# A gated three-branch layer: merge gates and branch projections from feature-major to token-major, and another order of the first transfers

## The chip, the cores and the metric

The kernel runs on one core of one Trainium2 chip. A core has TensorE (matmuls into the accumulators of PSUM), VectorE (DVE), ScalarE (ACT), GpSimd (POOL) and SyncE (SP), which here issues DMAs; 16 DMA engines move data between HBM and SBUF. The metric is the device time of one execution in microseconds (us). Several runs are taken, and their median is compared.

## The reference, cut to what matters

The layer has d = 1024 features and 256 tokens. After the input projection each branch has its output, the branches are projected, weighted by sigmoid gates and summed, and one more projection and a residual add follow.

```python
h = rms_norm(x, norm_g)
(qa, ka, va, ga, ub, vb, gb, qc, gc, ma, mb, mc) = split_cols(h @ w_in, IN_SPLITS)
out_a = moba_attention(qa, ka, va) * silu(ga)          # 6 heads of 128, causal
out_b = gmlp_spatial_gate(ub, vb, gmlp_ln_g, w_spatial, b_spatial) * silu(gb)
out_c = memory_cross_attention(qc, mem_n, w_mem_kv) * silu(gc)
y = (sigmoid(ma) * (out_a @ w_branch_a)                # ma, mb, mc: 1024 columns each
     + sigmoid(mb) * (out_b @ w_branch_b)
     + sigmoid(mc) * (out_c @ w_branch_c))
x = x + y @ w_out
return rms_norm(x, final_norm_g)
```

## The kernel before

All weights are float32. Each is split into two rounded parts, hi and lo, and a product is made of three matmuls, hi x hi, hi x lo and lo x hi (`mm3`, L271 to L274), which sum into one accumulator. Activations are split in the same way (hh and hl of x times its gain, nh and nl of the normalised x, ah/al, obh/obl, och/ocl of the branches, yh and yl of y).

The weights come as pieces of 1 MB (`raw`, three buffers), all from SP's queue, and one piece is two chunks of 128 x 1024. `split` makes a chunk's hi on ScalarE (L129) and its lo on VectorE (L133), three chunks ahead of their use (`LEAD`), into four buffers of each. The main loop (L765) runs over all chunks; in each step it lets small units of work in (`U.slot`, L60: a unit runs when its predecessors are done for `gap` chunks and its cost fits the room of each engine), splits a chunk, loads a piece and issues the chunk's matmuls. The order of the instructions on each engine is the order in which this loop writes them.

There are two kinds of chunk. A "fea" chunk (`mm_fea`, L335) makes 128 output features for all 256 tokens: the weights are the stationary operand, the activations move, and 24 matmuls are 256 wide. A "tok" chunk (`mm_tok`, L286) makes part of 512 output features for two token halves of 128: the activations are stationary, the weights move, 12 matmuls are 512 wide, and four chunks fill two accumulators. Before the change the values (`vvb`, three groups of four chunks) and the memory's values (`mv`) are tok chunks, and everything else in the input projection is fea: among it the merge gates, 24 chunks called `sig` (L256, L375). The branch projections (`mm_br`, L693) take two chunks for each 128 features j of y: the sums over six, six and four blocks of the three branches, 48 matmuls of 256; VectorE multiplies each sum by its gate (L710), POOL and VectorE add (L715), and `split2` makes yh and yl. The output projection (`mm_out`, L723) needs y with features on the partitions.

PSUM has eight banks here: four `acc`, for the chunks, and four `aux`, for the units and the end.

At the start x (transposed) and the first four chunks of weights come in blocks k = 0 to 7 of 768 columns (`load_st`, L156), the first one in two parts with the gains. ScalarE makes hi of each block (L236) and hh (L224; for k = 0 VectorE, L234), VectorE makes hl (L227) and lo (L240). Five passes over a zero tile (L186) run on TensorE before the first data. Behind these blocks SP asks for piece 2, for x token-major (`xk`, L173) and then for the further pieces. The row sums of squares of `xk` (`xsq`, L202), the root (`xrow`) and its broadcast over the partitions by a matmul with a diagonal (`xrms`, L219) come while chunks 4 to 7 run; the accumulators of the vvb groups wait for it, since their eviction (`evict_v`, L317) multiplies by it, and POOL then scales x for nh and nl (L410).

Of the kernel before, what the change touches and what calls it, by code (L numbers as in the profile page):

```python
# [78 lines left out]
def tile_hybrid_layer(ctx: ExitStack, tc: tile.TileContext, xw, memT, mem, x, fin_g, ln_g, w, w_sp, b_sp, rope, out):  # L81
# [73 lines left out]

    def load_st(k, a, b):  # L156
        o = 0 if k == 0 and a == 0 else NG + k * XW + a
        e = NG + k * XW + b
        d = 0 if k < 4 else NG + 4 * XW
        nc.sync.dma_start(st[k // 4][:, o - d:e - d], xw[:, o:e])  # L160
# [12 lines left out]
    nc.sync.dma_start(V["xk"], x)  # L173
# [10 lines left out]
    wp = bank()  # L184
    for i in range(5):
        nc.tensor.matmul(wp, warm[:, 0:128], warm, start=True, stop=True)  # L186
# [44 lines left out]
    for k in range(KD):  # L231
        c, a, g = k // 2, (k % 2) * 512, gain[:, k:k + 1]
        if k == 0:
            nc.vector.tensor_scalar(hh[:, k, :], x_k(k), g, None, op0=OP.mult)  # L234
        for o, e in (((0, 256), (256, 512)) if k == 0 else ((0, 512),)):
            nc.scalar.activation(hi[c][:, a + o:a + e], st_k(k, S + o, S + e), AF.Copy)  # L236
# [49 lines left out]
    def mm_tok(c):  # L286
        _, name, o, k0 = chunks[c]
        sh, sl = (V["mh"], V["ml"]) if name == "mv" else (hh, hl)
        if k0 == 0:
            acc[name, o] = [acc_bank(), acc_bank()]  # L290
        for i in range(2):
            k = k0 + i
            if c < 4:

                parts = (((hh, hi, 0, 256), (hh, hi, 256, 512)) if k == 0 else ((hh, hi, 0, 512),)) \
                    + ((hl, hi, 0, 512), (hh, lo, 0, 512))
                for n, (src, wt, a, b) in enumerate(parts):
                    for t in range(2):
                        nc.tensor.matmul(acc[name, o][t][:, a:b], src[:, k, tsl(t)],
                                         wt[c][:, i * 512 + a:i * 512 + b], start=k + n == 0,  # L300
                                         stop=k == KD - 1 and n == len(parts) - 1)
# [33 lines left out]
    def mm_fea(c):  # L335
# [28 lines left out]
        elif name in ("ga", "gc"):  # L364
            if h == 0:
                slot_tile(name, [128, HA if name == "ga" else HC, S], name)
            nc.scalar.activation(V[name][:, h, :], p, AF.Silu)
        elif name == "gb":
            g = sq_tile()
            nc.scalar.activation(g, p, AF.Silu)  # L370
            nc.gpsimd.tensor_tensor(V["ub"][:, h, :], V["ub"][:, h, :], g, OP.mult)
        else:
            if h % 12 == 0:
                slot_tile(f"sig{h // 12}", [128, 12, S], f"p{1 + h // 12}")
            nc.scalar.activation(V[f"sig{h // 12}"][:, h % 12, :], p, AF.Sigmoid)  # L375
# [315 lines left out]
    BR = [("a", k) for k in range(HA)] + [("b", k) for k in range(GB)] + [("c", k) for k in range(HC)]  # L691

    def mm_br(c):  # L693
        _, j, part = chunks[c]
        if j == 0 and part == 0:
# [3 lines left out]
        src = {"a": (V["ah"], V["al"], HA, 0), "b": (V["obh"], V["obl"], GB, 1),  # L699
               "c": (V["och"], V["ocl"], HC, 2)}  # L700
        for i in range(KD):
            br, k = BR[part * KD + i]
            sh, sl, n, gi = src[br]
            if k == 0:
                acc[br] = acc_bank()[:, 0:S]
            mm3(acc[br], hi[c][:, hsl(i)], lo[c][:, hsl(i)], sh[:, k, :], sl[:, k, :], k == 0, k == n - 1)
            if k == n - 1:
                s = gi * KD + j
                sig = V[f"sig{s // 12}"][:, s % 12, :]
                nc.vector.tensor_tensor(sig, acc[br], sig, OP.mult)  # L710
                if br == "a":
                    acc["y"] = sig
                else:
                    eng = nc.gpsimd if br == "b" else nc.vector
                    eng.tensor_tensor(sig, acc["y"], sig, OP.add)  # L715
                    acc["y"] = sig
        if part == 1:
            split2(acc["y"], V["yh"][:, j, :], V["yl"][:, j, :])

# [166 lines left out]
```

## Time and profile before

| | |
|---|---|
| median of 3 runs | 338.62 us (338.11 to 338.70) |
| the profiled execution | 338.83 us, span 337.1 us |
| moved by DMA | 62.98 MB, mean 187 GB/s |
| 24 sigmoid evictions (L375) | first at 196.5, last at 262.7 us, 0.383 us each |
| 24 products with the gates (L710) | from 265.2 to 308.8 us, 0.418 us each |
| matmuls of the gates and the branches | 40 chunks of 24, 256 wide |

The span runs from the first to the last instruction of the profiled execution. In the lists below a row of the timeline is start, duration, engine, line, operation and tiles, a count and, in brackets, how long the engine stood idle before and what ended that. Matmuls overlap: their cost is read from the distance between starts. Busy shares of PE say little for the same reason.

### The profile page before, as it was taken

The numbers are of one execution on the slowest core, as the hardware profiler recorded it, in microseconds if no ns is written. First come the engines' busy times: TensorE is split into PE (matmuls) and PEld (weight loads), VectorE is DVE, ScalarE is ACT, GpSimd is POOL, SyncE is SP. The second block draws the span as 40 slices with busy tenths as digits, with TensorE's granted clock in tenths as the row PEclk, the third lists the DMA queues.
The fourth block names the chain that finished last, engine by engine and source line by source line (L and its number), as shares of the span: only waits on it lengthen the run. The fifth ranks groups of instructions, "written<-read, shape, count | busy, mean of one in ns | idle before, by whom it ended". The sixth has DMA issues, their size and how long they took to land.

```text
span 337.1 us, 6042 instructions
## 1 busy us (share of the span) xinstructions
PE 328.1 (97%) x2461; PEld 313.9 (93%) x2461; DVE 223.1 (66%) x352; ACT 193.0 (57%) x334; POOL 45.8 (14%) x50
## 2 busy tenths in 40 slices
PE   7999999999999999999999999999999999999992
PEld 4886899999999999988999999999999999999882
DVE  3846949978957898678694655444444677776552
ACT  4859669657775666546964564444444452534333
POOL 0006410000001090100035420000000001011022
PEclk9999999999999999999999999999999999999998
DMA  7988993554443372543656246455454635455003
GB/s 238 406 355 294 372 350 131 192 202 160 165 157 127 124 252 64 199 152 135 246 160 232 93 159 192 183 172 206 145 230 143 231 125 192 183 172 203 3 0 124
DMA packets 10732, 62.98 MB, mean 187 GB/s; under 512 B 1200, under 2 KB 1584, under 8 KB 4176
## 3 DMA queue, kind: packets, MB, share of 16 engines
q1 hardware_dynamic: 10704, 62.60, 51.7%
q8 instruction: 19, 0.31, 0.4%
q14 instruction: 9, 0.07, 0.1%
HBM read 61.55 MB, written 1.05 MB: 186 GB/s over the span
## 4 chain that ended last, share of the span: by engine, by line
PE 89%; DMA 5%; ACT 3%; DVE 1%; issue 1%; SPq 0%; DVEq 0%; ACTq 0%
PE acc L272 26%; PE acc L274 26%; PE acc L273 26%; DMA raw<-in_w_dram 4%; PE aux L272 2%; PE aux L273 2%; PE aux L274 2%; DMA st<-in_xw_dram 2%; PE aux L461 1%; ACT hi L129 1%; PE aux L630 1%; ACT jx L202 0%; SPq L160 0%; PE aux L501 0%; PE aux L534 0%
## 5 line engine op out<-in xcount | busy, mean ns | idle before, releaser
L133 DVE TENSOR_TENSOR lo<-raw,hi 128x1024 fp32r<-128x1024 f32 x102 | 128.3, 1260 | 74.5 <-ACT hi L129 74.0
L272 PE MATMUL acc<-nh,hi 128*128 128x256 f32 x496 | 141.3, 285 | 0.0
L274 PE MATMUL acc<-nh,lo 128*128 128x256 f32 x496 | 140.6, 283 | 0.0
L273 PE MATMUL acc<-nl,hi 128*128 128x256 f32 x496 | 140.6, 283 | 0.0
L129 ACT ACTIVATE hi<-raw 128x1024 fp32r<-128x1024 f32 x102 | 107.3, 1053 | 15.2 <-PE aux L274 5.1
L273 PEld LDWEIGHTS acc<-nl,hi 128*128 128x128 f32 x496 | 95.3, 192 | 0.0
L272 PEld LDWEIGHTS acc<-nh,hi 128*128 128x128 f32 x496 | 95.3, 192 | 0.0
L274 PEld LDWEIGHTS acc<-nh,lo 128*128 128x128 f32 x496 | 95.2, 192 | 0.0
L375 ACT ACTIVATE sig<-acc 128x256 f32<-128x256 f32 x24 | 9.2, 383 | 35.2 <-PE acc L274 35.2
L142 ACT ACTIVATE yh<-sig 128x256 fp32r<-128x256 f32 x8 | 3.3, 418 | 23.3 <-DVE sig L715 23.3
L715 POOL TENSOR_TENSOR sig<-sig 128x256 f32<-128x256 f32 x4 | 3.0, 740 | 86.7 <-DVE sig L710 86.7
L639 POOL TENSOR_TENSOR qk<-qk,ga 128x512 f32<-128x512 f32 x3 | 4.0, 1332 | 71.7 <-ACT qk L535 71.7
L272 PE MATMUL acc<-obh,hi 128*128 128x256 f32 x48 | 13.6, 284 | 0.0
L274 PE MATMUL acc<-ah,lo 128*128 128x256 f32 x48 | 13.6, 284 | 0.0
L273 PE MATMUL acc<-al,hi 128*128 128x256 f32 x48 | 13.6, 284 | 0.0
L274 PE MATMUL acc<-obh,lo 128*128 128x256 f32 x48 | 13.6, 284 | 0.0
L272 PE MATMUL acc<-ah,hi 128*128 128x256 f32 x48 | 13.6, 284 | 0.0
L273 PE MATMUL acc<-obl,hi 128*128 128x256 f32 x48 | 13.6, 284 | 0.0
L272 PE MATMUL acc<-hi,hh 128*128 128x512 f32 x32 | 12.7, 397 | 0.6 <-ACT vb L332 0.6
L273 PE MATMUL acc<-lo,hh 128*128 128x512 f32 x32 | 12.5, 391 | 0.0
L274 PE MATMUL acc<-hi,hl 128*128 128x512 f32 x32 | 12.5, 390 | 0.0
L710 DVE TENSOR_TENSOR sig<-acc,sig 128x256 f32<-128x256 f32 x24 | 10.1, 420 | 2.4 <-PE acc L274 2.4
(196 smaller groups left out, 583.6 us busy)
## 6 DMA issues: line engine op xcount, KB each, us to landing
raw<-in_w_dram SPq DMA_DIRECT2D x50, 1024.0 KB, 4.8
st<-in_xw_dram SPq DMA_DIRECT2D x7, 384.0 KB, 6.4
raw<-in_w_dram SPq DMA_DIRECT2D x2, 512.0 KB, 9.7
xk<-in_x_dram SPq DMA_DIRECT2D x1, 1024.0 KB, 10.7
mt<-in_memT_dram SPq DMA_DIRECT2D x2, 512.0 KB, 6.9
mm<-in_mem_dram SPq DMA_DIRECT2D x2, 512.0 KB, 8.4
out_dram<-xk SPq DMA_DIRECT2D x2, 384.0 KB, 2.5
fing<-in_fin_g_dram SPq DMA_DIRECT2D x1, 512.0 KB, 5.8
```

The costliest lines, as they stand in the source:

```text
L129: nc.scalar.activation(hi[c][:, a:b], raw[c // 2][:, o + a:o + b], AF.Copy)
L133: nc.vector.tensor_tensor(lo[c][:, a:b], raw[c // 2][:, o + a:o + b], hi[c][:, a:b].bitcast(F32), OP.subtract)
L142: nc.scalar.activation(dh, src, AF.Copy)
L272: nc.tensor.matmul(p, s_hi, m_hi, start=first, stop=False)
L273: nc.tensor.matmul(p, s_hi, m_lo, start=False, stop=False)
L274: nc.tensor.matmul(p, s_lo, m_hi, start=False, stop=last)
L375: nc.scalar.activation(V[f"sig{h // 12}"][:, h % 12, :], p, AF.Sigmoid)
L461: nc.tensor.transpose(p[:, hsl(j)], src, ident)
L630: nc.tensor.matmul(pv[:, a, t, :], V["vb"][:, t, hsl(g)], wsp[:, g, :], start=True, stop=True)
L639: nc.gpsimd.tensor_tensor(src, src, g, OP.mult)
L710: nc.vector.tensor_tensor(sig, acc[br], sig, OP.mult)
L715: eng.tensor_tensor(sig, acc["y"], sig, OP.add)
```

## The change

It has two parts. In the first, the gates become six tok groups of four chunks, whose eviction is one sigmoid of 512 columns for each token half, and the branch projections become token-major as well: two halves of 512 features, eight chunks each, with two accumulators for each branch and 12 matmuls of 512 in a chunk. y then has tokens on the partitions; a new unit `y_split` turns it by transposes on TensorE, two units for each half, and splits it from PSUM. POOL takes no part in the sums any more. In the second part the first transfers are issued by SP and ScalarE in turn, the blocks lie one behind another in HBM, piece 3 is asked for ahead of `xk`, seven passes run instead of five, VectorE makes hh for k = 0 to 3, the third vvb group takes two aux banks, and the costs and gaps of three units change.

```diff
-    load_st(0, 0, S + 256)
-    load_st(0, S + 256, XW)
-    for k in range(1, KD):
-        load_st(k, 0, XW)
+    load_st(nc.sync, 0, 0, S + 256)
+    load_st(nc.scalar, 0, S + 256, XW)
+    load_st(nc.sync, 1, 0, XW)
+    load_st(nc.scalar, 2, 0, XW)
+    for k in range(3, KD):
+        load_st(nc.sync, k, 0, XW)
     raw_alloc(2)
     load_part(2, 0, CH)
     load_part(2, CH, PIECE)
+    load(3)
...
-    for i in range(5):
+    for i in range(7):
         nc.tensor.matmul(wp, warm[:, 0:128], warm, start=True, stop=True)
...
-        if k == 0:
+        if k < 4:
             nc.vector.tensor_scalar(hh[:, k, :], x_k(k), g, None, op0=OP.mult)
...
-        if k:
+        if k >= 4:
             gain_hi(x_k(k), g, hh[:, k, :])
...
-    chunks += [("fea", "sig", j) for j in range(3 * KD)]
+    for g in range(6):
+        chunks += [("tok", "sig", g, 2 * i) for i in range(4)]
     n_in = len(chunks)
-    for j in range(KD):
-        chunks += [("br", j, 0), ("br", j, 1)]
+    for half in range(2):
+        chunks += [("br", half, i) for i in range(KD)]
...
-            acc[name, o] = [acc_bank(), acc_bank()]
+            acc[name, o] = [bank(), bank()] if o == 1024 else [acc_bank(), acc_bank()]
...
+        elif k0 + 2 == KD and name == "sig":
+            for t in range(2):
+                if o == 0:
+                    slot_tile(f"sig{t}", [128, 6, 512], f"p{1 + t}")
+                nc.scalar.activation(V[f"sig{t}"][:, o, :], acc[name, o][t], AF.Sigmoid)
...
-            [128, D], F32, name="jx", tag=("och", "ocl")[t])), after=["c4"], gap=1, cost=(0, 0, 1.1, 0))
+            [128, D], F32, name="jx", tag=("och", "ocl")[t])), after=["c4"], gap=1, cost=(0, 0, 0.95, 0))
     U.add("xrow", lambda: (rms_rows(ssx, rstd), rms_diag(rstd, "x")), after=["xsq0", "xsq1"], gap=0,
-          cost=(0, 0.6, 0.3, 0))
-    U.add("xrms", lambda: rms_bcast("x"), after=["xrow"], gap=0, cost=(0.5, 0, 0.4, 0))
+          cost=(0, 0.6, 0.05, 0))
+    U.add("xrms", lambda: rms_bcast("x"), after=["xrow"], gap=1, cost=(0.5, 0, 0.4, 0))
...
+    def y_split(half, i):
+        p = bank()
+        transpose4(p, [V[f"sig{t}"][:, half, (2 * i + a) * 128:(2 * i + a + 1) * 128] for a in range(2) for t in range(2)])
+        k = 4 * half + 2 * i
+        split2(p.rearrange("p (k s) -> p k s", k=2), V["yh"][:, k:k + 2, :], V["yl"][:, k:k + 2, :])
...
-        for i in range(KD):
-            br, k = BR[part * KD + i]
+        for i in range(2):
+            br, k = BR[2 * part + i]
             sh, sl, n, gi = src[br]
             if k == 0:
-                acc[br] = acc_bank()[:, 0:S]
-            mm3(acc[br], hi[c][:, hsl(i)], lo[c][:, hsl(i)], sh[:, k, :], sl[:, k, :], k == 0, k == n - 1)
...
+                acc[br] = [acc_bank(), acc_bank()]
+            for t in range(2):
+                mm3(acc[br][t], sh[:, k, tsl(t)], sl[:, k, tsl(t)], hi[c][:, i * 512:(i + 1) * 512],
+                    lo[c][:, i * 512:(i + 1) * 512], k == 0, k == n - 1)
+        if k == n - 1:
+            for t in range(2):
+                y, sig = (V[f"sig{t}"][:, g + half, :] for g in (0, gi))
+                nc.vector.tensor_tensor(sig, acc[br][t], sig, OP.mult)
+                if br != "a":
+                    nc.vector.tensor_tensor(y, y, sig, OP.add)
+            if br == "c":
+                for i in range(2):
+                    U.add(f"yt{half}{i}", lambda half=half, i=i: y_split(half, i), after=[f"c{c}"], gap=2,
+                          cost=(0.44, 0.6, 0.6, 0))
...
-        if s % 2 == 1 and s // 2 + 2 < n_pieces:
+        if s % 2 == 1 and 3 < s // 2 + 2 < n_pieces:
             load(s // 2 + 2)
```

What this does to the order on the engines is shown at three places. The first is ScalarE from its first instruction; before:

```order
L183 ACT_TABLE_LOAD
L236 ACTIVATE hi<-st_72 128x256 x2
L236 ACTIVATE hi<-st_72 128x512
L224 ACTIVATE hh<-st_72 128x256
L236 ACTIVATE hi<-st_72 128x512
L224 ACTIVATE hh<-st_72 128x256
L236 ACTIVATE hi<-st_72 128x512
L224 ACTIVATE hh<-st_72 128x256
```

and of the change (st_72 is the tile of blocks 0 to 3, st_73 that of 4 to 7):

```order
L164 DMA st_72<-in_xw_dram 128x256
L164 DMA st_72<-in_xw_dram 128x768
L190 ACT_TABLE_LOAD
L243 ACTIVATE hi<-st_72 128x256 x2
L243 ACTIVATE hi<-st_72 128x512 x3
L243 ACTIVATE hi<-st_73 128x512
L231 ACTIVATE hh<-st_73,st_72 128x256
```

Two DMAs stand ahead of the table load, and the three hh of blocks 1 to 3 have left. The second place is ScalarE while chunks 1 to 7 run, from the hi of chunk 4 on; before:

```order
L129 ACTIVATE hi<-raw 128x1024 x4
L202 ACTIVATE jx,ssx<-xk 128x1024
L129 ACTIVATE hi<-raw 128x1024
L202 ACTIVATE jx,ssx<-xk 128x1024
L206 ACTIVATE rt<-ssx,eps 128x2
L129 ACTIVATE hi<-raw 128x1024
L221 ACTIVATE bc<-aux 128x256
```

and of the change:

```order
L130 ACTIVATE hi<-raw 128x1024 x4
L209 ACTIVATE jx,ssx<-xk 128x1024 x2
L213 ACTIVATE rt<-ssx,eps 128x2
L130 ACTIVATE hi<-raw 128x1024 x2
L228 ACTIVATE bc<-aux 128x256
```

Both sums of squares and the root now stand ahead of the hi of chunk 8, where the second stood behind it; the broadcast keeps its place. The third place is TensorE in the output projection of the change, at the end of its second chunk, where aux are the accumulators and sig_2443 and sig_2445 the gates of the two token halves, in which y is summed:

```order
L280 MATMUL aux<-hi,yh 128x512
L281 MATMUL aux<-lo,yh 128x512
L282 MATMUL aux<-hi,yl 128x512
L472 MATMUL aux<-ident,sig_2443 128x128
L472 MATMUL aux<-ident,sig_2445 128x128
L472 MATMUL aux<-ident,sig_2443 128x128
L472 MATMUL aux<-ident,sig_2445 128x128
L472 MATMUL aux<-ident,sig_2443 128x128
```

Eight transposes stand there, of the second half of y; eight of the first half stand in the same way behind the second chunk of the second half. Before, no transposes stood behind the attention's.

More of the change, by code (lines that the diff above doesn't have):

```diff
@@ L154, in st_k, with load_st @@
         return st[k // 4][:, o + a:o + b]
[L156 to L160, printed above, removed]
+    def load_st(queue, k, a, b):
+        o = 0 if k < 4 else -NG - 4 * XW
+        row, at = (NG + XW, 0) if k == 0 else (XW, 128 * (NG + k * XW))
+        a, b = (a and a + NG, b + NG) if k == 0 else (a, b)
+        src = bass.AP(tensor=xw.tensor, offset=xw.offset + at + a, ap=[[row, 128], [1, b - a]])
+        o += NG + k * XW if k else 0
+        queue.dma_start(st[k // 4][:, o + a:o + b], src)
     def x_k(k):
         return st_k(k, 0, S)
-    load_st(0, 0, S + 256)
-    load_st(0, S + 256, XW)
-    for k in range(1, KD):
-        load_st(k, 0, XW)
+    load_st(nc.sync, 0, 0, S + 256)
[4 more added lines that the diff above has]
+        load_st(nc.sync, k, 0, XW)
     raw_alloc(2)
@@ L287, in mm_tok @@
         _, name, o, k0 = chunks[c]
-        sh, sl = (V["mh"], V["ml"]) if name == "mv" else (hh, hl)
+        sh, sl = {"mv": ("mh", "ml"), "sig": ("nh", "nl")}.get(name, (None, None))
+        sh, sl = (V[sh], V[sl]) if sh else (hh, hl)
         if k0 == 0:
-            acc[name, o] = [acc_bank(), acc_bank()]
+            acc[name, o] = [bank(), bank()] if o == 1024 else [acc_bank(), acc_bank()]
         for i in range(2):
@@ L371, in mm_fea @@
             nc.gpsimd.tensor_tensor(V["ub"][:, h, :], V["ub"][:, h, :], g, OP.mult)
[L372 to L375, printed above, removed]
         U.done[f"{name}{h}"] = now[0]
@@ L691, in tile_hybrid_layer @@
     BR = [("a", k) for k in range(HA)] + [("b", k) for k in range(GB)] + [("c", k) for k in range(HC)]
+    def y_split(half, i):
[3 more added lines that the diff above has]
+        split2(p.rearrange("p (k s) -> p k s", k=2), V["yh"][:, k:k + 2, :], V["yl"][:, k:k + 2, :])
     def mm_br(c):
-        _, j, part = chunks[c]
-        if j == 0 and part == 0:
+        _, half, part = chunks[c]
+        if half == 0 and part == 0:
             nc.scalar.preload_act_table(AF.Sqrt)
@@ L698, in mm_br @@
             slot_tile("yl", [128, KD, S], "nl", F32R)
-        src = {"a": (V["ah"], V["al"], HA, 0), "b": (V["obh"], V["obl"], GB, 1),
-               "c": (V["och"], V["ocl"], HC, 2)}
-        for i in range(KD):
-            br, k = BR[part * KD + i]
+        src = {"a": (V["ah"], V["al"], HA, 0), "b": (V["obh"], V["obl"], GB, 2),
+               "c": (V["och"], V["ocl"], HC, 4)}
+        for i in range(2):
+            br, k = BR[2 * part + i]
             sh, sl, n, gi = src[br]
             if k == 0:
-                acc[br] = acc_bank()[:, 0:S]
-            mm3(acc[br], hi[c][:, hsl(i)], lo[c][:, hsl(i)], sh[:, k, :], sl[:, k, :], k == 0, k == n - 1)
[L707 to L718, printed above, removed]
+                acc[br] = [acc_bank(), acc_bank()]
[12 more added lines that the diff above has]
+                          cost=(0.44, 0.6, 0.6, 0))
     ss = const.tile([128, 2, 4], F32, name="ss")
@@ L844 @@
     br = np.concatenate([np.asarray(w_branch_a)[0], np.asarray(w_branch_b)[0], np.asarray(w_branch_c)[0]], axis=0)
-    br = br.reshape(16, 128, KD, 128).transpose(2, 1, 0, 3)
+    br = br.reshape(4, 4, 128, 2, 512).transpose(3, 0, 2, 1, 4)
     wo = np.asarray(w_out)[0].reshape(2, 4, 128, 2, 512).transpose(0, 3, 2, 1, 4)
@@ L848 @@
         tok(np.concatenate([col["va"], col["vb"]], axis=1)), fea(qk), fea(col["qc"]), fea(wkv[:, :CW]),
-        tok(wkv[:, CW:]), fea(col["gc"]), fea(col["gb"]), fea(col["ma"]),
-        fea(col["mb"]), fea(col["mc"]), br.reshape(-1), wo.reshape(-1)])
+        tok(wkv[:, CW:]), fea(col["gc"]), fea(col["gb"]),
+        tok(np.concatenate([col["ma"], col["mb"], col["mc"]], axis=1)), br.reshape(-1), wo.reshape(-1)])
+    gains = np.concatenate([np.asarray(norm_g)[0].reshape(KD, 128).T, np.asarray(mem_norm_g)[0].reshape(KD, 128).T],
+                           axis=1)
     first = w[:2 * 128 * PIECE].reshape(2, 128, 4, 512).transpose(1, 0, 2, 3).reshape(128, KD, 512)
     xw = np.concatenate([tr(x), first], axis=2)
+    xw = [np.concatenate([gains, xw[:, 0]], axis=1)] + [xw[:, k] for k in range(1, KD)]
     pos = np.arange(S, dtype=np.float32)
@@ L860 @@
     rope = np.stack([np.concatenate([cs, cs]), np.concatenate([-sn, sn])], axis=1)
-    gains = np.concatenate([np.asarray(norm_g)[0].reshape(KD, 128).T, np.asarray(mem_norm_g)[0].reshape(KD, 128).T],
-                           axis=1)
     arrays = {
-        "xw": np.concatenate([gains, xw.reshape(128, -1)], axis=1),
+        "xw": np.concatenate([a.reshape(-1) for a in xw]),
         "memT": np.ascontiguousarray(tr(mem)),
```

## The prediction

> **What bounds the kernel now.** First the page: span, busy shares, the chain that ended last.
>
> ```profile
> span 337.1 us, 6042 instructions
> PE 328.1 (97%) x2461; PEld 313.9 (93%) x2461; DVE 223.1 (66%) x352; ACT 193.0 (57%) x334; POOL 45.8 (14%) x50
> ...
> PE 89%; DMA 5%; ACT 3%; DVE 1%; issue 1%; SPq 0%; DVEq 0%; ACTq 0%
> ```
>
> TensorE ends the kernel almost everywhere; DMA and ScalarE have their shares of the chain in the first 32 us. The profiled execution took 338.83 us, 1.73 more than its span; the median of the runs is 338.62, so 0.2 comes off at the end. An edit counts if it shortens the row of matmuls or a hole in it. A matmul's printed duration is no price, since matmuls overlap; the price is the distance between two starts. The timeline of TensorE in the gate stage (columns: start, duration):
>
> ```profile
> 215.69 0.28 PE L272 MATMUL acc<-nh,hi 128*128 128x256 f32 x1
> 215.81 0.28 PE L273 MATMUL acc<-nl,hi 128*128 128x256 f32 x1
> ```
>
> A 256-wide matmul costs 0.120 us, so a chunk of 24 takes 2.88. The gates' evictions confirm it over the whole stage:
>
> ```profile
> L375 ACT ACTIVATE sig<-acc x24: 383/383/383, 196.5 to 262.7; 128x256 f32<-128x256 f32 x24
> ```
>
> (262.7 - 196.5) / 23 = 2.88: no hole anywhere. Token-major chunks, with 12 matmuls of 512, stand in three places; two whole ones:
>
> ```profile
> 18.40 0.39 PE L272 MATMUL acc<-hi,hh 128*128 128x512 f32 x1
> 18.63 0.39 PE L273 MATMUL acc<-lo,hh 128*128 128x512 f32 x1
> ...
> 21.12 0.39 PE L272 MATMUL acc<-hi,hh 128*128 128x512 f32 x1
> ```
>
> ```profile
> 151.57 0.39 PE L272 MATMUL acc<-hi,mh 128*128 128x512 f32 x1
> ...
> 154.33 0.38 PE L461 MATMUL aux<-ident,p 128*128 128x128 f32 x2
> ```
>
> One took 2.72 (0.227 a matmul), the other 2.76. The same products cost less in 512-wide passes: 2 x 0.120 = 0.240 against 0.227 to 0.230.
>
> **The change, term 1: 40 chunks token-major.** 24 gate chunks and 16 branch chunks go from 2.88 us to between 2.72 and 2.76. I take 2.73, near the first row, whose neighbours are quiet: 40 x 0.15 = **-6.0 us** (bounds -6.4 and -4.8). What each chunk needs from others stays: 512 KB of weights, one hi, one lo.
>
> A rule of the Trainium skill speaks against this term (TensorE: Matmul & The Clock Gate, section Back-to-back issue gap): the gap of warm matmuls is N/2.4 + 2.5 ns, 109.2 at 256 and 215.8 at 512, so that halving the count saves 2.5 ns a pair. As an estimate from that page the term would be 40 x 12 x 2.5 ns = -1.2 us. The trace does not agree: 120 and 227 ns.
>
> **Term 2: y must be turned.** y is now token-major, and the output projection wants it feature-major: 16 transposes on TensorE, in two blocks of eight (after the second chunk of the second half, and after the second output chunk). The chain of waits before (start, share of the chain in us) has such a block:
>
> ```profile
> 171.34 0.87 PE aux L461 x8
> ```
>
> 0.87 a block, **+1.7 us**. They wait for nobody: y's last sum has two chunks (5.5 us) before them. Of the work beside it, VectorE's is largest:
>
> ```profile
> 309.33 0.43 DVE L715 TENSOR_TENSOR sig<-sig 128x256 f32<-128x256 f32 x1
> ...
> 320.95 1.23 DVE L133 TENSOR_TENSOR lo<-raw,hi 128x1024 fp32r<-128x1024 f32 x1 [1.55 <-ACT hi L129]
> 322.60 0.69 DVE L736 TENSOR_TENSOR xk<-aux,xk 128x512 f32<-128x512 f32 x1 [0.43 <-PE aux L274]
> ...
> 323.33 0.63 ACT L738 ACTIVATE jk<-xk 128x512 f32<-128x512 f32 x1 [2.41 <-DVE xk L736]
> ```
>
> Per half there are 12 operations of 512 (6 products, 4 sums, 2 lo parts of y) at 0.69, and 8 lo of 1.23: 18.1 us, against 22.7 us on TensorE. An accumulator pair is read within 2.1 us and wanted again two chunks later. One new wait has little room: at the third output chunk the half bank (1,1,256) takes a bank of the second pair of transposes, and waits for their yl. By these rows (0.63 for a yh, 0.69 for a yl, two of each, the first yh beside the last transposes) both yl end 1.9 us behind the block; the bank is wanted after six matmuls of 512 and six of 256, 2.2 us behind it. I take 0 (0 to +0.3). The dropped POOL sums wait for nobody and cost nothing.
>
> **Term 3: two holes near 30 us.** TensorE's timeline:
>
> ```profile
> 26.34 0.39 PE L274 MATMUL acc<-hi,hl 128*128 128x512 f32 x1
> 26.94 0.71 PE L219 MATMUL aux<-dg,ones 128*128 128x128 f32 x4 [0.22 <-DVE dg L212]
> ...
> 30.68 0.39 PE L274 MATMUL acc<-hi,hl 128*128 128x512 f32 x1
> 31.69 0.51 PE L272 MATMUL acc<-hi,hh 128*128 128x512 f32 x1 [0.62 <-ACT vb L332]
> ```
>
> The second is 1.01 - 0.23 = 0.78 us: the third vvb group wants the accumulators of the first two, whose evictions ended late. It now takes two of the four aux banks, where only the warm-up's and the broadcast's were taken: **-0.8 us** (bounds -0.8 and 0). The first is 0.60 - 0.23 = 0.37 us, the wait for the diagonal of rstd, which is now made a chunk earlier. What could be late is x itself, whose transfer now comes behind raw 3:
>
> ```profile
> xk<-in_x_dram SPq DMA_DIRECT2D x1, 1024.0 KB, 10.7
> ```
>
> ```profile
> 0.80 4.38 SPq L160 DMA_DIRECT2D st<-in_xw_dram  x9
> ...
> 7.67 0.33 SPq L173 DMA_DIRECT2D xk<-in_x_dram  x1
> 8.62 16.12 SPq L117 DMA_DIRECT2D raw<-in_w_dram  x4
> ```
>
> ```profile
> 20.93 2.01 ACT L129 ACTIVATE hi<-raw 128x1024 fp32r<-128x1024 f32 x2 [3.92 <-DMA raw<-in_w_dram]
> ...
> 24.84 1.04 ACT L202 ACTIVATE jx<-xk 128x1024 f32<-128x1024 f32 x1
> ```
>
> x landed at 18.4 and raw 3 at 20.9; they change places. From the second square's start to the diagonal's matmul it was 2.1 us (24.84 to 26.94); from 20.9, with a first square of 1.04 ahead, that gives 24.1; chunk 6 (counted from 0) ends near 24.9 by term 4. So **-0.4 us** with 0.8 us to spare (bounds -0.4 and, were x a microsecond later still, -0.2). Queued behind the squares on ScalarE is the hi of chunk 8, on VectorE its lo; both have until 27.6. On SP the rest of the order stands. The swap is needed besides: raw 3's lo parts ended thus,
>
> ```profile
> 22.03 2.36 DVE L133 TENSOR_TENSOR lo<-raw,hi 128x1024 fp32r<-128x1024 f32 x2 [3.75 <-ACT hi L129]
> ```
>
> the one for chunk 6 near 23.2, and chunk 6 now starts near 22.1; with raw 3 in x's place it is ready near 20.7. Last, the normalised x:
>
> ```profile
> 28.16 8.02 POOL L410 TENSOR_TENSOR st<-st,bc 128x256 f32<-128x256 f32 x8 [26.79 <-ACT bc L221]
> ```
>
> POOL needs 8.0 us for its eight blocks, from 25.6 now; nh and nl follow in step, the last near 39, and chunk 12 wants them one k after the other from 38.7 to 41.2. The last has 2 us to spare; I cost it at nothing.
>
> **Term 4: the start.** Warm-up, first products, the clock's rise, the DMA:
>
> ```profile
> 1.25 2.32 PE L186 MATMUL aux<-warm 128*128 128x512 bf16 x5 [1.25 <-DVE warm L176]
> 4.11 1.68 PE L299 MATMUL acc<-hi,hh 128*128 128x256 f32 x4 [0.54 <-ACT hi L236]
> ...
> 9.00 1.06 PE L299 MATMUL acc<-lo,hh 128*128 128x512 f32 x2
> 9.85 0.98 PE L299 MATMUL acc<-hi,hh 128*128 128x512 f32 x2
> 10.67 0.62 PE L299 MATMUL acc<-hi,hl 128*128 128x512 f32 x2
> 11.13 0.63 PE L299 MATMUL acc<-lo,hh 128*128 128x512 f32 x2
> ```
>
> Each row holds two matmuls. Up to 9.85 they start 0.85 / 2 = 0.427 us apart, behind 10.67 at 0.46 / 2 = 0.23: full speed begins near 10.5, though the row PEclk prints 9 from the first slice. The last holes before it lie at 3.6 to 4.1 (shown) and near 4.9, where the second half of k = 0 came:
>
> ```profile
> 0.80 1.28 ACT L183 ACT_TABLE_LOAD   x1 [0.80 <-PEq L875]
> ...
> 3.61 0.42 ACT L236 ACTIVATE hi<-st 128x256 fp32r<-128x256 f32 x1 [1.53 <-DMA st<-in_xw_dram]
> 3.61 0.35 DVE L234 TENSOR_SCALAR hh<-st 128x256 fp32r<-128x256 f32 x1 [2.27 <-DMA st<-in_xw_dram]
> ...
> 4.52 0.42 ACT L236 ACTIVATE hi<-st 128x256 fp32r<-128x256 f32 x1 [0.50 <-DMA st<-in_xw_dram]
> ...
> 14.66 1.06 ACT L129 ACTIVATE hi<-raw 128x1024 fp32r<-128x1024 f32 x1 [0.63 <-DMA raw<-in_w_dram]
> ```
>
> So the rise came 5.6 us after the last hole. Seven passes reach to 1.25 + 7 x 0.427 = 4.24, past the first products' data (3.61 + 0.42 = 4.03), and that second half is now asked for by ScalarE at once, not one issue of SP later (4.38 / 9 = 0.49 us): no hole. Counted from 1.25, 5.6 us give a rise near 6.9. Then 2.66 / 0.427 = 6.2 of the 48 passes run slowly and 41.8 x 0.227 = 9.5 us follow: the fourth chunk ends at 16.4 instead of 18.40. The next chunk's second matmul (before: 18.63) needs the lo of raw 2, which was ready at 14.66 + 1.06 + 1.26 = 17.0, that is -1.6; with transfers one issue earlier some -2.0. I take **-1.7 us**. If the clock rises where it did, only the holes' 0.2 goes: bounds -0.2 and -2.2. VectorE's three more hh, 0.35 each, stand beside TensorE's 1.4 to 2.6 us per k and cost nothing. ScalarE's two DMA issues, at SP's 0.49, push its table load of 1.28 from 0.8 to 1.8, to end near 3.1, before the first data at 3.6.
>
> The Trainium skill (TensorE: Matmul & The Clock Gate, section What's actually happening) has the clock rise after one busy window of about 3.4 us in a free-running row of windows. The trace agrees with such a rise between 3.4 and 6.8 us after the last hole; by the rule the rise would now fall between 4.7 and 8.1 and shift from run to run, and the term, estimated from that page, would be -1.5 to -2.0.
>
> **Sum.** 338.83 - 6.0 + 1.7 - 0.8 - 0.4 - 1.7 = 331.6; less 0.2 for the median gives **331.4 us**.
>
> **The rivals.**
> (a) *The start gives nothing.* The engines of the DMA are at 0.93 of their time already in the fourth microsecond, so the k = 1 block, which now shares them with k = 2, lands later; a new hole at 6.8 us puts the rise back to 10.5. For it speaks this row:
>
> ```profile
> 3.00:4.00 1.00, 0.57 (x2) 0.00 (x0) 0.35 (x2) 0.39 (x1) 0.00 (x0) 1.00 0.93 217
> ```
>
> Against it: 217 GB/s in a stretch with idle issue slots. Term 4 is then -0.2: 332.9 us. Chance 0.22.
> (b) *Wide matmuls cost more here than at 18 us,* with ScalarE and VectorE beside them: a token chunk takes 2.85, a saving of 0.03, and term 1 is -1.2: 336.2 us. Against it: at 151 us, with both engines at work, it took 2.76. Chance 0.03. By the gap rule of the Trainium skill (TensorE: Matmul & The Clock Gate, Back-to-back issue gap) the time would be the same.
> (c) *Slower: VectorE bounds the branch stage.* TensorE has 22.7 us a half, VectorE needs 18.1. It decides from 0.69 + 4.6 / 12 = 1.07 us per operation of 512; at 1.40 each half takes 4 us more, and 331.4 + 8 = 339.4 us. The rows give 0.69, and 0.43 for 256: chance 0.02.
>
> **Chances.** The forecast has 0.70, (a) 0.22, (b) 0.03, (c) 0.02; 0.03 stay for mixtures, all faster but 0.01. About 0.2% is what a measurement of this kernel can tell from no change. Faster by more: 0.95; within: 0.02; slower: 0.03. The range takes in (a), most of the bounds of term 1 on one side and of term 4 on the other: 330.4 to 333.4.
>
> **What would show it.** Gate chunks every 2.73 us, 10.9 for each pair of sigmoids; branch chunks alike; two blocks of eight transposes at 0.87; no hole at the third vvb group nor at the diagonal; starts 0.227 apart from near 7 us; the fifth chunk at 16.7. The forecast is wrong if the 512 starts lie above 0.235 apart in the gate stage, if the clock rises near 10 us, or if TensorE waits for VectorE between the branch chunks.

## The result and the profile after

The changed kernel takes 331.09 us (median; three runs at 330.89, 330.97 and 331.21; a fourth was disturbed, 827.2 us, and only shifts this median by 0.1). The kernel before took 338.66 us beside it. The ratio is 0.9778, with a 95% interval of 0.9758 to 0.9797: faster. The forecast was 331.4 us, in a range of 330.4 to 333.4.

The page of the changed kernel: span, busy shares, and the chain that ended last.

```profile
span 329.1 us, 5062 instructions
PE 321.7 (98%) x1999; PEld 289.3 (88%) x1999; DVE 222.9 (68%) x339; ACT 191.2 (58%) x315; POOL 39.7 (12%) x42
...
PE 97%; DVE 1%; ACT 0%; issue 0%; DVEq 0%
```

The DMA's 5% and ScalarE's 3% have left the chain, and TensorE has 462 matmuls fewer. To see where the 8 us went, the starts of the same stages stand side by side; each is the start of the stage's first matmul.

| stage begins (us) | before | after | change of the stretch that ends there |
|---|---|---|---|
| first product | 4.11 | 4.43 | +0.32 (within the next row) |
| fifth chunk (chunk 4) | 18.40 | 16.52 | -1.88 from the span's start on |
| chunk 12 | 42.06 | 38.76 | holes near 30 us -1.42 |
| gates | 193.31 | 190.00 | -0.01 |
| branches | 262.49 | 255.41 | gates -3.77 |
| output projection | 308.57 | 299.83 | branches -2.53, transposes +0.87 |
| last matmul | 330.59 | 322.73 | +0.88, of it transposes +0.87 |
| span | 337.10 | 329.14 | -7.96 in all |

**Gates.** The first row of the stage before, and of the changed kernel:

```profile
193.31 0.36 PE L272 MATMUL acc<-nh,hi 128*128 128x256 f32 x1
```

```profile
190.00 0.48 PE L280 MATMUL acc<-hi,nh 128*128 128x512 f32 x1
```

The timeline of TensorE (start, duration) in a gate chunk, and the row of the sigmoids (count: shortest, median and longest in ns, first and last start):

```profile
200.34 0.39 PE L280 MATMUL acc<-hi,nh 128*128 128x512 f32 x1
200.56 0.39 PE L281 MATMUL acc<-lo,nh 128*128 128x512 f32 x1
200.79 0.39 PE L282 MATMUL acc<-hi,nl 128*128 128x512 f32 x1
```

```profile
L322 ACT ACTIVATE sig<-acc x12: 593/598/602, 200.9 to 255.6; 128x512 f32<-128x512 f32 x12
```

The starts are 0.225 to 0.23 apart; of the gate stage's matmuls nearly all stand 226 or 227 ns from the next. Twelve of them make 2.72 us, and a group of four chunks 10.88. The sigmoid that ends the second group starts at 212.09, the last one at 255.61: 43.52 us for four groups, so there is no hole in the stage.

**Transposes.** The two blocks of eight in the chain of waits (start, share of the chain), and the timeline behind the second one:

```profile
282.79 0.87 PE aux L472 x8
305.45 0.87 PE aux L472 x8
```

```profile
306.55 1.29 DVE L144 TENSOR_TENSOR yl<-aux,yh 128x512 fp32r<-128x512 f32 x2 [1.48 <-ACT yh L143]
...
308.13 0.28 PE L282 MATMUL acc<-hi,yl 128*128 128x256 f32 x1
...
308.25 0.28 PE L280 MATMUL aux<-hi,yh 128*128 128x256 f32 x1
```

yl ends at 306.55 + 1.29 = 307.84, and the bank that the output projection takes from it is first written at 308.25, 0.12 behind its predecessor: the new wait costs nothing, with 0.4 us to spare.

**The holes near 30 us.** TensorE at the diagonal and at the third vvb group:

```profile
24.45 0.40 PE L282 MATMUL acc<-hi,hl 128*128 128x512 f32 x1
...
24.69 0.61 PE L226 MATMUL aux<-dg,ones 128*128 128x128 f32 x4
...
25.05 0.47 PE L280 MATMUL acc<-hi,hh 128*128 128x512 f32 x1
...
27.66 0.39 PE L282 MATMUL acc<-hi,hl 128*128 128x512 f32 x1
27.88 0.39 PE L280 MATMUL aux<-hi,hh 128*128 128x512 f32 x1
```

The diagonal's four matmuls follow 0.24 behind the product before them, and the group on aux starts 0.22 behind the last one on acc. Both holes are gone.

**The start.** Each row below holds two matmuls or more, as the count says:

```profile
1.25 3.17 PE L193 MATMUL aux<-warm 128*128 128x512 bf16 x7 [1.25 <-DVE warm L183]
4.43 1.19 PE L309 MATMUL acc<-hi,hh 128*128 128x256 f32 x4
5.42 0.94 PE L309 MATMUL acc<-hi,hl 128*128 128x512 f32 x2
6.20 0.63 PE L309 MATMUL acc<-lo,hh 128*128 128x512 f32 x2
6.84 0.73 PE L309 MATMUL acc<-hi,hh 128*128 128x512 f32 x2
7.41 0.62 PE L309 MATMUL acc<-hi,hl 128*128 128x512 f32 x2
```

Full speed begins at about 6.1 us: from 5.42 to 6.20 two matmuls take 0.78, one slow distance of 0.43 and one of 0.35 in which the clock rises, and behind 7.41 they take 0.46. The transfers moved as well, by more than the forecast had. The hi of piece 2's first chunk, which waits for its transfer, stood at 14.66 before:

```profile
12.73 1.06 ACT L130 ACTIVATE hi<-raw 128x1024 fp32r<-128x1024 f32 x1 [0.68 <-DMA raw<-in_w_dram]
```

### The profile page after: what moved, and what is told of

Its sections match the earlier page's. It is cut to its first block, busy times and chain, and to the rows that moved or that the text cites. A ratio compares the mean times of both kernels' runs of the same rounds, so it can differ in the third digit from the quotient of the medians.

```text
span 329.1 us, 5062 instructions
## 1 busy us (share of the span) xinstructions
PE 321.7 (98%) x1999; PEld 289.3 (88%) x1999; DVE 222.9 (68%) x339; ACT 191.2 (58%) x315; POOL 39.7 (12%) x42
## 3 DMA queue, kind: packets, MB, share of 16 engines
HBM read 61.55 MB, written 1.05 MB: 190 GB/s over the span
## 4 chain that ended last, share of the span: by engine, by line
PE 97%; DVE 1%; ACT 0%; issue 0%; DVEq 0%
PE acc L280 26%; PE acc L282 26%; PE acc L281 26%; PE acc L309 4%; PE aux L280 3%; PE aux L282 3%; PE aux L281 3%; PE aux L472 2%; PE aux L193 1%; PE aux L641 1%; PE aux L512 0%; PE aux L545 0%; ACT jk L757 0%; PE aux L226 0%; DVE xk L755 0%; DVE xk L777 0%
## 5 line engine op out<-in xcount | busy, mean ns | idle before, releaser
L280 PE MATMUL acc<-nh,hi 128*128 128x256 f32 x304 | 86.6, 285 | 0.0
L282 PE MATMUL acc<-nh,lo 128*128 128x256 f32 x304 | 86.0, 283 | 0.0
L281 PE MATMUL acc<-nl,hi 128*128 128x256 f32 x304 | 85.9, 283 | 0.0
L281 PEld LDWEIGHTS acc<-nl,hi 128*128 128x128 f32 x304 | 58.2, 192 | 0.0
L280 PEld LDWEIGHTS acc<-nh,hi 128*128 128x128 f32 x304 | 58.2, 191 | 0.0
L282 PEld LDWEIGHTS acc<-nh,lo 128*128 128x128 f32 x304 | 58.2, 191 | 0.0
L280 PE MATMUL acc<-hi,nh 128*128 128x512 f32 x96 | 37.5, 390 | 0.0
L282 PE MATMUL acc<-hi,nl 128*128 128x512 f32 x96 | 37.4, 389 | 0.0
L281 PE MATMUL acc<-lo,nh 128*128 128x512 f32 x96 | 37.3, 389 | 0.0
L282 PEld LDWEIGHTS acc<-hi,nl 128*128 128x128 f32 x96 | 18.0, 188 | 3.8
```

Of the source, the lines that this page charges most:

```text
L280: nc.tensor.matmul(p, s_hi, m_hi, start=first, stop=False)
L281: nc.tensor.matmul(p, s_hi, m_lo, start=False, stop=False)
L282: nc.tensor.matmul(p, s_lo, m_hi, start=False, stop=last)
```

## The experiments

All of them are edits of the changed kernel, each in three rounds beside runs of the kernel before. An interval of a ratio is 0.004 to 0.006 wide, 1.3 to 2.1 us, so the smaller effects are read in the profiles. "Chunk 4" is the fifth chunk; the clock's rise is read from the distances between TensorE's starts, as above.

### The two parts apart

The first kernel keeps the token-major gates and branches alone and takes everything else back (five passes, SP alone, the old layout, hh by ScalarE, acc banks, x ahead of piece 3, the old costs and gaps). The second keeps those and takes the gates and branches back.

```diff
-    for g in range(6):
-        chunks += [("tok", "sig", g, 2 * i) for i in range(4)]
+    chunks += [("fea", "sig", j) for j in range(3 * KD)]
...
-    for half in range(2):
-        chunks += [("br", half, i) for i in range(KD)]
+    for j in range(KD):
+        chunks += [("br", j, 0), ("br", j, 1)]
```

(These are the second kernel's main lines; `mm_br`, `mm_tok`, `mm_fea` and the order of the weights go back with them.)

> The gates and branches token-major, everything of the second part (start, layout, piece 3, accumulators, costs) as before the change. Theory: the parts add up without acting on one another; between the two profiles the gates and branches gave -6.24 us and the two blocks of transposes +1.74, so 338.7 - 4.5 = 334.2 us, a chunk every 2.72 us in gates and branches, and the fifth chunk starts at 18.4 us as before. Rival: part of the gate stage's gain comes from the earlier transfers, not from the wide matmuls; then chunks of 2.8 us or more, and 335.5 us or more.

> The second part alone: start, layout, piece 3, accumulators, costs and gaps as in the change, gates and branches feature-major as before. Theory: -1.88 us at the start and -1.42 at the two holes near 30 us stay to the end: 338.7 - 3.3 = 335.4 us; gate chunks every 2.88 us. Rival: the time won at the start is given back later, since the weights or the normalised x come no earlier; then 336.5 us or more, with new holes on TensorE behind 30 us.

Token-major alone took 334.38 us against 338.92 (ratio 0.9869, 0.9845 to 0.9894), the second part alone 335.44 (0.9899, 0.9879 to 0.9920). That is -4.5 and -3.5 us; the sum of -8.0 stands beside -7.6 for the whole change, within the spread of the runs (those of before reach from 338.26 to 339.55). In the first profile the gates took 65.42 us, in that of the whole change 65.41: they gain nothing from earlier transfers. In the second they took 69.19, as before (69.18), and no new hole appeared behind 30 us. Both rivals fall. In one point the first expectation missed: the fifth chunk started at 17.53, not at 18.4, since the clock rose earlier than in the kernel before (below); the profiled run is the fastest of its four, 333.67. The first profile has the two holes back:

```profile
26.42 0.71 PE L222 MATMUL aux<-dg,ones 128*128 128x128 f32 x4 [0.57 <-DVE dg L215]
...
31.16 0.50 PE L276 MATMUL acc<-hi,hh 128*128 128x512 f32 x1 [0.62 <-ACT vb L343]
```

### What a wide matmul saves

```diff
-                mm3(acc[name, o][t], sh[:, k, tsl(t)], sl[:, k, tsl(t)], hi[c][:, i * 512:(i + 1) * 512],
-                    lo[c][:, i * 512:(i + 1) * 512], k == 0, k == KD - 1)
+                for n in ((0, 256), (256, 512)) if name == "sig" else ((0, 512),):
+                    mm3(acc[name, o][t][:, n[0]:n[1]], sh[:, k, tsl(t)], sl[:, k, tsl(t)],
+                        hi[c][:, i * 512 + n[0]:i * 512 + n[1]], lo[c][:, i * 512 + n[0]:i * 512 + n[1]],
+                        k == 0 and n[0] == 0, k == KD - 1 and n[1] == 512)
```

> The changed kernel with each matmul of 512 in the 24 gate chunks made as two of 256 with the same stationary tile, operands and accumulator otherwise alike. Theory A (what the wide matmul saves is a cost of each matmul, 0.240 - 0.227 = 13 ns): gate chunks every 2.88 us again, 24 x 0.155 = +3.7 us, 334.8 us. Theory B (the gain is in which operand moves or in the evictions, not in the count): chunks stay at 2.72 to 2.76, time 331.1 to 331.9. A page of the Trainium skill (TensorE: Matmul & The Clock Gate, Back-to-back issue gap) has 2.5 ns a matmul, which as an estimate from that page would be +0.7 us.

It took 334.36 us (ratio 0.9866, 0.9840 to 0.9892), 3.3 more than the changed kernel, and the gate stage 69.19 us instead of 65.41. TensorE's timeline:

```profile
201.05 0.28 PE L282 MATMUL acc<-hi,nl 128*128 128x256 f32 x1
201.17 0.28 PE L280 MATMUL acc<-hi,nh 128*128 128x256 f32 x1
201.29 0.28 PE L281 MATMUL acc<-lo,nh 128*128 128x256 f32 x1
```

The distance is 0.120 again, with the wide evictions and the moving weights kept: theory A. The saving belongs to the number of matmuls, 240 - 227 = 13 ns for each one dropped. Every matmul here brings its own weight load (the changed kernel's page counts 1999 of each), so whether the 13 ns are the matmul's or the load's is not shown. By the 2.5 ns of the Trainium skill (TensorE: Matmul & The Clock Gate, section Back-to-back issue gap) the stage would have lost 0.7 us, as an estimate; it lost 3.8. That section gives its figure for a matmul in isolation and says that in a stream of weight loads and matmuls both set the spacing, so its figure is not one for this kernel.

### The passes and the clock

```diff
-    for i in range(7):
+    for i in range(5):
```

A second kernel has eight.

> The changed kernel with five warm-up passes instead of seven. Theory A (the clock rises a fixed 5 us or so after the last long hole of TensorE): five passes end near 3.6, the first data is there at 4.4, and this hole of 0.8 us puts the rise from 6.1 to between 9 and 10; the fifth chunk starts 1.3 to 1.8 us later than 16.5, and the time is near 332.5 us. Theory B (earlier data brought the rise, whatever the passes): rise within 0.5 us of 6.1, time 331.1 +- 0.3. Theory C, by a page's rule in a sentence of its own: the Trainium skill (TensorE: Matmul & The Clock Gate, What's actually happening) has a free-running row of windows of about 3.4 us, by which the rise would come in steps and shift from run to run.

> The changed kernel with eight warm-up passes. The clock's rise stood at 6.1, 6.7 and 6.75 us in three profiles with seven passes, at 10.4, 7.5 and 10.5 in three with five. Theory A (a free-running window in which TensorE has to be busy all through): with eight passes the row from 1.25 has no hole above 0.1 us, the rise falls somewhere between 4.7 and 8.2 and shifts from run to run; the first product starts at 4.7 instead of 4.43, time 331.1 +- 0.4. Theory B (a fixed time after the last hole): rise 4.9 to 5.5 us after 1.25, as with seven, in every profile.

With five passes it took 331.86 us (331.39 to 332.44; ratio 0.9795, 0.9774 to 0.9816), with eight 330.83 (330.36 to 331.79; 0.9764, 0.9733 to 0.9796). The intervals don't separate these from the changed kernel; the profiles say more. With five passes, in its slowest run:

```profile
1.25 2.32 PE L193 MATMUL aux<-warm 128*128 128x512 bf16 x5 [1.25 <-DVE warm L183]
4.23 1.19 PE L309 MATMUL acc<-hi,hh 128*128 128x256 f32 x4 [0.66 <-ACT hi L243]
...
6.93 1.07 PE L309 MATMUL acc<-hi,hh 128*128 128x512 f32 x2
7.80 1.05 PE L309 MATMUL acc<-hi,hl 128*128 128x512 f32 x2
8.66 1.05 PE L309 MATMUL acc<-lo,hh 128*128 128x512 f32 x2
```

TensorE is still slow at 8.66; the rise comes near 10.4, and chunk 4 starts at 18.14 instead of 16.52. So a hole ahead of the first product can cost 1.6 us. But a fixed time behind the last hole is not the rule. The kernel with token-major alone has five passes too, and a hole of 0.5 us before 7.39 besides:

```profile
6.04 1.05 PE L305 MATMUL acc<-lo,hh 128*128 128x512 f32 x2
7.39 0.78 PE L305 MATMUL acc<-hi,hh 128*128 128x512 f32 x2 [0.29 <-ACT hh L227]
8.00 0.64 PE L305 MATMUL acc<-hi,hl 128*128 128x512 f32 x2
```

Its clock rises at about 7.6, right behind that hole. With eight passes full speed was there by 4.8, 3.5 us after the first pass. Over the eleven profiles with seven or eight passes the rise lay between 4.4 and 6.8 us, while the first pass always started at 1.25. A row of windows that runs on without regard to the kernel would give such a spread. The Trainium skill has it so (TensorE: Matmul & The Clock Gate, section What's actually happening); its window of about 3.4 us would put the rise between 4.7 and 8.1. The runs agree but for 0.3 us at the lower end, though none of the eleven lies in the last 1.3 us of that range, so windows are not shown to be the cause. How large a hole a window bears was not settled: with five passes the hole ahead of the first product put the rise back to 10.4 in one profile and, with a second hole behind it, only to 7.6 in another.

### The transfers

```diff
-    load_st(nc.scalar, 0, S + 256, XW)
+    load_st(nc.sync, 0, S + 256, XW)
...
-    load_st(nc.scalar, 2, 0, XW)
+    load_st(nc.sync, 2, 0, XW)
```

> The changed kernel with all first transfers issued by SP; the blocks one behind another in HBM as in the change. The transfers of the changed kernel land some 2 us earlier than before (raw 2 whole at 13.90 instead of 15.85). Theory A: the second issuing engine brings this; then the k blocks land near the times of before (k = 7 near 13, raw 2 near 15.9), the fifth chunk starts 1 to 2 us later, time 332 to 333. Theory B: the layout brings it; then k = 7 lands within 0.6 us of 11.0 and the time is within 0.5 us of the changed kernel's 331.1.

The kernel with the old layout keeps both engines and takes its blocks from rows 24 KB apart.

> The changed kernel with the old layout of x and the first weights in HBM (a block is 128 rows of 3 KB, 24 KB apart, not one contiguous run); SP and ScalarE issue as in the change. With one queue and the new layout k = 7 landed at 12.26 and raw 2 whole at 15.66, with two engines at 11.00 and 13.90. Theory A (the second engine brings the transfers' advance): k = 7 near 11.0, raw 2 near 13.9, time within 0.4 us of the changed kernel. Theory B (the layout has a share of its own): 0.5 us or more later on both, time still within 0.5 us since the transfers have some 1.3 us to spare.

The one queue took 331.28 us (ratio 0.9780, 0.9760 to 0.9800), the old layout 330.97 (0.9766, 0.9736 to 0.9796): the same time as the changed kernel. For the one queue theory A had the later transfers right and the time wrong. The transfers are not the same. The rows are the window from 3 to 5 us (the last two columns: share of the DMA engines, GB/s) of the kernel before, the changed kernel, one queue, and the old layout:

```profile
3.00:5.00 2.00, 1.34 (x5) 0.51 (x3) 0.86 (x3) 0.83 (x2) 0.00 (x0) 1.00 0.92 275
```

```profile
3.00:5.00 2.00, 1.99 (x7) 0.84 (x6) 1.04 (x3) 0.72 (x2) 0.00 (x0) 1.00 1.05 385
```

```profile
3.00:5.00 2.00, 2.00 (x8) 1.10 (x7) 1.30 (x3) 0.72 (x2) 0.00 (x0) 1.00 0.91 258
```

```profile
3.00:5.00 2.00, 1.87 (x6) 0.72 (x5) 0.91 (x3) 0.72 (x2) 0.00 (x0) 1.00 0.94 329
```

With one queue the DMA engines are nearly as busy (0.91 against 1.05), yet move a third less, and piece 2's hi starts 1.76 us later than in the changed kernel; with the old layout it starts 0.39 later:

```profile
14.49 1.06 ACT L130 ACTIVATE hi<-raw 128x1024 fp32r<-128x1024 f32 x1 [1.18 <-DMA raw<-in_w_dram]
```

```profile
13.12 1.06 ACT L130 ACTIVATE hi<-raw 128x1024 fp32r<-128x1024 f32 x1 [0.33 <-DMA raw<-in_w_dram]
```

So the second engine brings the transfers' advance; a share of the layout, 0.4 to 0.7 us, is within what they shift between profiles. The 1.9 us of this pair is the upper end: piece 2's hi started between 12.7 and 13.7 in the eleven profiles with two engines, 13.2 in the mean, and at 14.15, 14.49 and 14.66 in the three with SP alone, so the second engine is worth about 1.3 us. The Trainium skill says that several issuing engines save only the time of issuing (DMA: Bandwidth & Descriptors, section Issuing engines are not separate DMA queues). Here SP's issues of the nine blocks took 4.68 us alone and 3.63 with ScalarE's help, and these transfers gained more than that 1.05; the rate between 3 and 5 us differs although six of the nine blocks were issued by 3.6 with one queue, 1.97 MB, of which 0.82 had come by 5 us.

Why the time is the same: in the changed kernel nothing waits for piece 2. With one queue TensorE does, for its lo at chunk 4's second matmul, but only 0.25 us:

```profile
16.39 0.39 PE L280 MATMUL acc<-hi,hh 128*128 128x512 f32 x1
16.87 0.50 PE L281 MATMUL acc<-lo,hh 128*128 128x512 f32 x1
```

### hh by ScalarE

```diff
-        if k < 4:
+        if k == 0:
             nc.vector.tensor_scalar(hh[:, k, :], x_k(k), g, None, op0=OP.mult)
...
-        if k >= 4:
+        if k:
             gain_hi(x_k(k), g, hh[:, k, :])
```

> The changed kernel with hh of blocks k = 1 to 3 by ScalarE as before the change. Theory: ScalarE then makes hi and hh of a block one after the other, hh is late by its 0.4 us, and the small hole before the products of k = 1 (0.29 us in the changed kernel) grows to 0.7; +0.4 us where the transfers don't take it up, so 331.1 to 331.6; the rise of the clock falls anywhere between 5 and 8.5 us. Rival: hh by VectorE gains nothing, since hh of k = 1 is ready with hi by either engine: no hole above 0.3 us, time 331.1 +- 0.2.

It took 331.45 us (ratio 0.9778, 0.9752 to 0.9803). The first of the next rows is ScalarE's hi for k = 1, which starts when the block lands, the last TensorE's first product with it:

```profile
5.90 0.63 ACT L243 ACTIVATE hi<-st 128x512 fp32r<-128x512 f32 x1 [1.40 <-DMA st<-in_xw_dram]
6.44 0.49 ACT L231 ACTIVATE hh<-st 128x256 fp32r<-128x256 f32 x1
```

```profile
6.98 0.73 PE L309 MATMUL acc<-hi,hh 128*128 128x512 f32 x2 [0.94 <-ACT hh L231]
```

From the landing to the product it is 1.08 us; in the changed kernel 6.84 - 6.15 = 0.69, with this row:

```profile
6.15 1.67 ACT L243 ACTIVATE hi<-st 128x512 fp32r<-128x512 f32 x3 [1.50 <-DMA st<-in_xw_dram]
```

The theory's 0.4 us at k = 1 is there, though the times (331.45 and 331.09) don't separate it. The hole itself, some 1.1 us, is wider than expected, since the clock rose at 4.4 in this run and TensorE was done early with k = 0.

### The accumulators and piece 3

```diff
-            acc[name, o] = [bank(), bank()] if o == 1024 else [acc_bank(), acc_bank()]
+            acc[name, o] = [acc_bank(), acc_bank()]
```

> The changed kernel with the third vvb group on the acc banks again. In the changed kernel this group starts at 27.88 us, and the last eviction of the second group, for which it waited before, ends at 28.77 + 0.51 = 29.28. Theory A (the wait returns, and larger than before, since the broadcast now comes later against the chunks): a hole of 1.4 us, 331.1 + 1.4 = 332.5 us. Theory B (the term as the prediction has it): 0.8 us, 331.9. Rival: the accumulators are free in time with the earlier diagonal, no hole, 331.1.

It took 331.46 us (ratio 0.9779, 0.9755 to 0.9803); from chunk 4 to chunk 12 it is 23.15 us against 22.24, +0.91, part of which an earlier chunk 4 (16.12) hides in the total. The timeline:

```profile
27.93 0.39 PE L282 MATMUL acc<-hi,hl 128*128 128x512 f32 x1
...
28.37 0.51 ACT L347 ACTIVATE vb<-acc,rstd 128x256 f32<-128x256 f32 x1
...
28.94 0.50 PE L280 MATMUL acc<-hi,hh 128*128 128x512 f32 x1 [0.61 <-ACT vb L347]
```

The hole is 1.01 - 0.23 = 0.78 us, as in the prediction (theory B). Theory A failed because three matmuls into the group's first accumulator go ahead, and only the second waits.

```diff
-    load(3)
...
-        if s % 2 == 1 and 3 < s // 2 + 2 < n_pieces:
+        if s % 2 == 1 and s // 2 + 2 < n_pieces:
```

> The changed kernel with x (token-major) asked for ahead of piece 3 again. The prediction held that piece 3 had to come first, since its lo would end near 23.2 us and its first chunk starts near 22.1. In the changed kernel all transfers land 2 us earlier; piece 3 behind x would land at 18.9, its first lo end at 18.9 + 1.06 + 1.26 = 21.2, and the chunk starts at 22.0. Theory A: no hole, 331.1 +- 0.3, the swap isn't needed. Theory B (as the prediction has it, or lo queued behind other work of VectorE): a hole of 0.5 to 1.1 us at the chunk's second matmul, 331.6 to 332.2.

It took 330.97 us (330.60 to 331.33; ratio 0.9760, 0.9736 to 0.9784). In its profile, where the transfers were 1 us later than in the changed kernel's (piece 3 landed at 19.9, not at 18.9 as expected), chunk 6 waits for its lo:

```profile
22.03 0.39 PE L279 MATMUL acc<-hi,hh 128*128 128x512 f32 x1
22.38 0.19 PEld L280 LDWEIGHTS acc<-lo,hh 128*128 128x128 f32 x1 [0.39 <-DVE lo L134]
```

0.35 - 0.23 = 0.12, and 0.11 more at the next matmul: 0.24 us. The diagonal is late too, by a little: its weight load waits for dg, and its four matmuls take 0.47 us, not 0.36.

```profile
25.07 0.52 PEld L225 LDWEIGHTS aux<-dg,ones 128*128 128x128 f32 x4 [0.29 <-DVE dg L218]
```

From chunk 4 to chunk 12 it is 22.65 us against 22.24: the swap is worth 0.41 in this profile, whose transfers are the latest of all with two engines. The median, 330.97, shows nothing of it.

### Another order of the first transfers

TensorE might wait less for k = 1 if that block shared the DMA engines with nothing, or with one that is wanted later. The first kernel leaves ScalarE the second half of k = 0 alone; the second, whose diff this is, gives it k = 3 too.

```diff
-    load_st(nc.scalar, 2, 0, XW)
-    for k in range(3, KD):
+    load_st(nc.sync, 2, 0, XW)
+    load_st(nc.scalar, 3, 0, XW)
+    for k in range(4, KD):
```

> The changed kernel with the k = 2 block issued by SP behind k = 1, so that ScalarE issues the second half of k = 0 alone. In profiles with two queues k = 1 and k = 2 land within 0.3 us of one another, k = 1 at 5.7 to 6.1, and where the clock rises early TensorE waits for it: holes of 0.2 to 0.9 us near 6 us. Theory A (k = 1 and k = 2 share the engines): k = 1 lands near 5.2 to 5.5, k = 2 near 6.5, the hole goes, 330.4 to 330.9. Theory B (one queue alone brings 220 to 300 GB/s up to 6 us): k = 1 no earlier than 5.7, k = 2 near 7, time 331.1 +- 0.4.

> As the run before, with k = 3 issued by ScalarE right behind the second half of k = 0; SP issues k = 1, k = 2 and the rest. Theory A (two queues fill the engines whatever they carry, and k = 3 is wanted last of the three): k = 1 lands near 5.7, k = 2 near 6.7, k = 3 before 7, raw 2 whole near 13.9, time 330.6 to 331.1. Theory B (k = 3 takes the engines from k = 1): k = 1 later than 6.1, a hole of 0.5 us or more, 331.1 to 331.6.

The first took 330.68 us (330.36 to 331.32; ratio 0.9758, 0.9735 to 0.9780), the second 330.50 (330.38 to 330.77; 0.9751, 0.9732 to 0.9771). All four runs of the second lie below the changed kernel's fastest, but the intervals overlap: 0.6 us, likely, not settled. In the first, k = 1 landed at 4.82 (theory A had 5.2 to 5.5) and its hole went, but k = 2 then came at 7.35, not at 6.5, and TensorE waited for it:

```profile
8.06 0.73 PE L309 MATMUL acc<-hi,hh 128*128 128x512 f32 x2 [0.26 <-ACT hi L243]
```

In the second TensorE waits for k = 1 alone, since the clock rose at 4.4, and for nothing behind it:

```profile
6.55 0.73 PE L310 MATMUL acc<-hi,hh 128*128 128x512 f32 x2 [0.55 <-ACT hi L244]
7.12 0.63 PE L310 MATMUL acc<-hi,hl 128*128 128x512 f32 x2
```

## Why the prediction came out

**Term 1, -6.0, measured -6.30** (gates -3.77, branches -2.53). The 40 chunks cost 2.72 us each, the lower of the two rows that it chose from. The doubled matmuls show the cause. Rival (b) is out, and so is the gap rule for these matmuls.

**Term 2, +1.7, measured +1.74.** Two blocks of 0.87, and the wait at the output bank is 0. Rival (c) is out: VectorE's sums took 0.69 us for 512 columns as assumed, and between the branch chunks TensorE waits nowhere (no distance above 0.24 us but the 0.31 behind the transposes).

**Term 3, -1.2, measured -1.42.** Right in both places. What is missing in the sum is 0.1 us behind each hole: the second matmul after a hole came 0.11 late, so the two were worth 0.47 and 0.88. The reason given for the swap of piece 3 and x failed in part: "needed besides" was worked out with the old landing times, and the transfers came 1 to 2 us earlier; taking the swap back cost 0.41 us in its profile and nothing in the median. Which edit took away the hole at the diagonal is not settled: no run has the new costs and gaps alone.

**Term 4, -1.7, measured -1.88.** The size is right, and four of its steps are not, so that luck has a part in it. "Counted from 1.25, 5.6 us give a rise near 6.9": it was 6.1 in the profiled run, and nothing counts from the last hole; the rise falls anywhere between 4.4 and 6.8. "No hole": the first data landed 0.3 us later (first product at 4.43), and the products of k = 1 began about 0.3 us late, for which rival (a) has a mechanism, the block that shares the engines with k = 2. It landed at 6.13 instead of 5.80, but in the three profiles with SP alone it landed between 5.76 and 6.29, so the mechanism is not shown; and the consequence failed, since the rise did not move back. And "transfers one issue earlier", 0.4 to 0.5 us, was 1.9 to 2 in this profile. So the wait that set the -1.7, for the lo of piece 2 at 17.0, did not come: that lo was made from 14.39 to 15.61 and wanted at 16.75, and TensorE's own row, which the prediction let end at 16.4, decided. The steps make up for one another: an early rise meets the wait for k = 1, a late one costs slow matmuls, and in all eleven profiles chunk 4 started between 16.1 and 16.9. Of the edits at the start only the number of passes moved the time noticeably when it was taken back alone: by 0.8 us in the median and 1.6 in the profile, against -0.1 to +0.4 for the second queue, the layout and hh. That the passes are what the start gained by is likely, then, but not clear of the noise.

**The sum.** The terms measured give -7.86, the rest -0.10, which lies behind the last matmul.

## What to carry to other kernels

Where TensorE is the bound and a product can run either way round, count the matmuls: each one dropped was worth 13 ns here, with its weight load, and turning the result back cost 0.11 us for each 128 x 128 tile; so it pays for outputs that nobody needs turned (the gates, -3.8 us) and little for those that must be (the branches, -2.5 + 1.7). Keep TensorE without a hole from its first pass to its first product: the passes don't bring the rise of the clock at a set time, but a hole can put it back by several microseconds, in some profiles and not in others. When a transfer starts earlier, work out anew the landing of everything behind it, before another edit is justified by the old times.

## What was not expected of the hardware

- Two engines that issue DMAs moved 378 to 404 GB/s between 3 and 5 us in the profiles where each has a whole block of 384 KB early and the blocks are contiguous, one engine 258 to 275 in the profiles where SP issues alone, with DMA engines busy at 0.91 or more in both; 329 where ScalarE issued only 128 KB, and 329 with the strided layout.
- The clock's rise moves by 2.4 us between profiles of kernels whose TensorE starts alike, and the row PEclk shows nothing of the slow phase.
- TensorE is late once more behind a hole: the second matmul of 512 behind a hole came 0.11 us late (22.38 to 22.72 with x ahead), and behind a block of plain float32 matmuls (diagonal, transposes) 0.08 to 0.09 us, without a hole (25.05 to 25.37 in the changed kernel).
